# Two exponent arrays and two attention matrices for the heads of branch A, and another order of projections

## The chip, the cores and the metric

The kernel runs on one core of one Trainium2 chip. The metric is the device time of one execution in microseconds, taken as the median of several runs. The engines are named as the profile names them: PE (TensorE) for matmuls, PEld for its weight loads, DVE (VectorE), ACT (ScalarE), POOL (GpSimd) and SP, which issues most transfers.

## The reference

The kernel computes a trunk of two layers over 512 positions of width 1024, in float32. In each layer three branches share one input projection, and a squared-ReLU MLP follows:

```
z  = rms_norm(x) @ w_in          # columns for all branches
A: 4 heads of a gated linear recurrence, forward and backward, state 128 x 128
   log_f, key = gates(z_f, lower bound);  attn[t, s] = sum_k q[t] key[s] exp(b[t] - b[s])
B: u * (W_s @ layer_norm(v) + b_s) in 128-position chunks, 4 groups
C: 8 query heads, 2 key heads, windowed attention |i - j| <= 128, partial rotary, sink logit
merged = sum over branches of sigmoid(gate) * (y_branch @ w_br)
x = x + merged @ w_out;  x = x + relu(rms_norm(x) @ w_up)^2 @ w_down
```

## The kernel before, in words

Everything is tiled to 128 partitions by 512 columns. A float32 product is made from three float32r matmuls: each operand is split in a high and a low part, and high-high, low-high and high-low are added up in PSUM (`mm3`, lines 212 to 214). A weight chunk of 128x1024 is fetched by SP into one of two buffers (tag "wr", line 187), cast to its high part by ACT (line 207) and its low part is made by DVE (line 208). One projection (`proj`) is eight such triples, 24 matmuls, and DVE empties its PSUM bank with a multiplication by the row norm (`evac`, line 708, and line 717 for the gates of a head). Projections use tag "m", two PSUM banks.

The program is written as a trace of operations. A planner with a model of the engines puts them in order: an operation written earlier goes first, `hp()` moves one ahead, and `with later(n)` counts it as if it were written n operations later. Each engine then works through its list in order. Tiles of one tag share a fixed number of buffers, and a new tile waits until one is free.

In each layer a first part multiplies the normed input with the columns that all branches share (`seven`, lines 418 to 420). Then comes the branch stage, which the change is about. Its parts:

- Branch A. `a_ffb(h)` projects the two gates of head h (two projections `f`), then `a_gates` makes an array `ex` of four rows of 128x512: exponents, written by lines 531 and 532 in layer 0, 540 and 548 in layer 1. `a_head` works through seven levels of block size. In each one ACT takes exponentials of `ex` into `qt` (line 572) and `kt` (line 575), DVE multiplies `qt` with the query (line 573), PE forms four 128x128 products (line 558), the result goes into the attention matrix `at` by a masked copy (DVE, line 563) or a copy (ACT, lines 578 and 592), and two additions on DVE update `ex` for the next level (line 600). Behind the levels come the states between chunks (`kd`, `kT`, `stp`, `qd`, lines 606 to 632; line 629 is the last reader of `ex`), the output matmuls (line 643), a norm and a transpose (line 655). `qt`, `kt`, `dg`, `kd`, `qd`, `asq` and `ao` share tag "a" with three buffers. Queries share tag "q" with two.
- Head 0 keeps its `ex` in a four-row tile outside the branch pool (`Z4`), and heads 1 to 3 share one buffer of tag "ex". All heads share one buffer of `at`.
- Branch C projects keys, values and four query groups (`ck`, `cv`, `cq`), rotates them (`rot`: DVE lines 916, 917, 919 and POOL line 918), splits the queries (ACT line 946, DVE line 947), and then runs 16 blocks: scores on PE (lines 963, 964), row maximum, exponentials (ACT line 970), scaling, transposes (`pT`, line 992) and output (`po`, line 997, copied by line 999).
- Branch B ends in eight gate projections `gz` with the projection `yB` beside them (`merge_b(d)`; `fill` calls it with `later(30000)`). They are the work that PE does when nothing else is ready; so are the four output gates `ag` of branch A and the projection `yC` of branch C's output (lines 254 to 256).

The order in which these are written is:

```
ck, cv, cq x4  ->  c_run(0)  ->  head(1): f, f, q and the head  ->  c_run(1..3)
-> fill(0,1,2) -> head(2) -> fill(3,4) -> head(3) -> fill(5,6,7) -> ag x4, yC
```

`c_run` is counted 15000 operations later, `fill` and what follows it 30000. Head 0 is written ahead of all this, its gates already in the part before the stage.

Of the kernel before, what the change touches and what calls it, by code (L numbers as in the profile page):

```python
# [6 lines left out]
F32 = mybir.dt.float32  # L7
# [5 lines left out]
P = 128  # L13
S = 512
# [46 lines left out]
def trunk(tc, xT, xt, ws, vec, fnb, bsb, snk, wst, rope, cmask, amask, ident, out):  # L61
    nc = tc.nc
# [25 lines left out]
    part = {}  # L88
# [4 lines left out]
    def nm(s):  # L93
        ctr[0] += 1
        return f"{s}_{ctr[0]}"

    def T(tag, name, dt=F32):
        where = part[HOME[tag]] if tag in HOME else sb
        return where.tile([P, S], dt, tag=tag, bufs=SLOTS[tag], name=nm(name))
# [11 lines left out]
    def Z4(name):  # L111
        z4[:] = [sb.tile([P, 4, S], F32, tag="z4", bufs=1, name=nm(name)), 0]
        return z4[0]
# [397 lines left out]

    def a_gates(l, h, z2, lbs):

        if h == 0:

            ex, e = Z4("ex"), [T("zt", "ga") for _ in range(2)]
            both = [(e[d], z2[d]) for d in range(2)]
        else:
            ex, e = part["br"].tile([P, 4, S], F32, tag="ex", bufs=1, name=nm("ex")), Z2("ga")
            both = [(e, z2)]  # L520
            e, z2 = [e[:, 0], e[:, 1]], [z2[:, 0], z2[:, 1]]
        lfo = [ex[:, 3], ex[:, 1]]
        for e_, z_ in both:
            nc.scalar.activation(e_, z_, AF.Abs)
        for e_, z_ in both:
            nc.scalar.activation(e_, e_, AF.Exp, scale=-1.0)
        for e_, z_ in both:
            nc.scalar.activation(e_, e_, AF.Ln, bias=onep_t[:, 0:1])
        if l == 0:
            for d in range(2):  # L530
                nc.vector.scalar_tensor_tensor(lfo[d], z2[d], 0.0, e[d], ALU.min, ALU.subtract)
                nc.vector.tensor_tensor(ex[:, 2 * d], lfo[d], z2[d], ALU.subtract)
        else:
            l1p, llb, dl = lbs
            u = e
            for e_, z_ in both:
                nc.vector.scalar_tensor_tensor(e_, z_, 0.0, e_, ALU.min, ALU.subtract)
            for d in range(2):
                c = slice(d * 4 + h, d * 4 + h + 1)
                nc.vector.scalar_tensor_tensor(ex[:, 2 * d], u[d], l1p[:, c], z2[d], ALU.add, ALU.subtract)  # L540
                nc.scalar.activation(z2[d], u[d], AF.Abs, bias=dl[:, c])
                nc.vector.tensor_scalar(u[d], u[d], l1p[:, c], llb[:, c], ALU.add, ALU.max)
            for e_, z_ in both:
                nc.scalar.activation(z_, z_, AF.Exp, scale=-1.0)
            for e_, z_ in both:
                nc.scalar.activation(z_, z_, AF.Ln, bias=onep_t[:, 0:1])
            for d in range(2):
                nc.vector.tensor_tensor(lfo[d], u[d], z2[d], ALU.add)
        return ex

    def a_head(l, h, ex, q, vt):
        at = part["br"].tile([P, 4, P], F32, tag="at", bufs=1, name=nm("at"))

        def attn(kk, qq):
            pt = PT("a", "at")
# [146 lines left out]
    for l in range(DEPTH):  # L702
# [217 lines left out]
            return z  # L920


        lo64, hi64 = slice(0, 64), slice(64, 128)
        ck = evac(proj(xs, "ck", l, "ck"), "ch", "ck")
        cvT = evac(proj(xs, "cv", l, "cv"), "ch", "cv")
# [96 lines left out]
                        c_out(*prev)  # L1022
                    prev = cur

        def head(h):
            g = a_ffb(h)
            q = evac(proj(xs, "q", l, "q", h), "q", "q")
            oa.append(a_head(l, h, g, q, vt))

        prev = None  # L1030
        c_run(0)
        head(1)
        c_run(1)
        c_run(2)
        c_run(3)
        fill(0,1,2)
        with later(15000):
            c_out(*prev)
        head(2)
        fill(3,4)  # L1040
        head(3)
        fill(5,6,7)
        with later(30000):
            for h in range(4):
                gate_a()
# [270 lines left out]
```

## Time and profile before

| | |
|---|---|
| runs, median (lowest to highest) | 1730.86 us (1730.69 to 1731.39), 3 runs |
| profiled execution, span from first to last instruction | 1729.5 us |
| profiled execution's own time | not on the page beside the span; the median of the runs is 1.4 us above the span |
| mean granted clock of TensorE | 0.996 |
| branch stage, layer 0 | about 164 to 448 us |
| branch stage, layer 1 | about 1024 to 1306 us |

Times in the profile count from the first instruction. A line of the timeline gives start, length, engine, line of the code, operation, output and inputs, and in brackets how long the engine stood idle before it and what ended that. A line of the waits gives who waited for whom, the total, how often, and the longest. In the table by stage each engine's busy time stands with its number of instructions in brackets. A matmul's length there includes the time in which it overlaps the next one.

### The profile page before, as it was taken

The page shows a single profiled execution, that of the slowest core. Times are in us where ns is not written, and L with a number is a line of the kernel's source. Part 1 is how long each engine was busy: PE and PEld are TensorE (multiplying, and loading weights), DVE is VectorE, ACT ScalarE, POOL GpSimd, SP SyncE. Part 2 cuts the span into 40 slices and gives each one's busy share as a digit, 9 for nine tenths or more (in the row PEclk, how much of TensorE's full clock was granted, in tenths as well). Part 3 has the DMA queues.
Part 4 walks back from the last instruction along what each step waited for, and adds up shares of the span by engine and source line. Part 5 has one row for each costly group of instructions (what it writes and reads, how often), then busy time and mean ns, then how long its engine had stood idle before and what let it go on. Part 6 is the DMA issues. An engine that isn't in the chain of part 4 may idle for free.

```text
span 1729.5 us, 21976 instructions
## 1 busy us (share of the span) xinstructions
PE 1685.3 (97%) x8024; PEld 1405.0 (81%) x8024; DVE 1297.1 (75%) x2009; ACT 1017.1 (59%) x1715; POOL 146.1 (8%) x215
## 2 busy tenths in 40 slices
PE   8999999999999999999999999999999999999997
PEld 7888878887877888888888787888877878888886
DVE  7996977687566668686889869876776567686867
ACT  7665567677335555545665754877772355545454
POOL 0011200000310000000010112000004000000001
PEclk9999999999999999999999999999999999999999
DMA  8342232231545332233423422322317353232311
GB/s 331 98 146 92 83 104 81 72 104 55 203 187 182 98 110 98 98 98 98 134 92 126 147 93 71 104 79 75 111 48 273 130 182 98 98 98 97 119 65 49
DMA packets 58283, 200.04 MB, mean 116 GB/s; under 512 B 7904, under 2 KB 8288, under 8 KB 58176
## 3 DMA queue, kind: packets, MB, share of 16 engines
q1 hardware_dynamic: 44640, 154.72, 26.6%
q0 software_dynamic: 13248, 43.40, 6.7%
q8 instruction: 63, 1.03, 0.3%
q10 hardware_dynamic: 288, 0.52, 0.1%
q14 instruction: 44, 0.36, 0.1%
HBM read 177.64 MB, written 20.97 MB: 115 GB/s over the span
## 4 chain that ended last, share of the span: by engine, by line
PE 43%; issue 20%; DVE 4%; ACT 2%; POOL 0%; POOLq 0%; ACTq 0%; DVEq 0%
PE up L213 3%; PE up L212 3%; PE up L214 3%; PE dA L418 2%; PE dA L420 2%; PE dA L419 2%; PE at L558 1%; PE gA L418 1%; PE gz L214 1%; PE gz L213 1%; PE gz L212 1%; PE dC L418 1%; PE dC L420 1%; PE dC L419 1%; PE gA L420 1%
## 5 line engine op out<-in xcount | busy, mean ns | idle before, releaser
L207 ACT CAST wh<-wq 128x1024 fp32r<-128x1024 f32 x201 | 211.4, 1052 | 208.2 <-PE up L213 49.3
L208 DVE TENSOR_TENSOR wl<-wq,wh 128x1024 fp32r<-128x1024 f32 x201 | 245.1, 1222 | 117.1 <-ACT wh L207 116.1
L208 DVE TENSOR_TENSOR wl<-wr,wh 128x1024 fp32r<-128x1024 f32 x166 | 203.9, 1228 | 148.0 <-ACT wh L207 147.6
L207 ACT CAST wh<-wr 128x1024 fp32r<-128x1024 f32 x166 | 174.0, 1049 | 214.6 <-PE up L213 67.3
L212 PE MATMUL up<-xh,wh 128*128 128x512 f32 x512 | 199.2, 390 | 1.9 <-ACT u L1171 1.9
L213 PE MATMUL up<-xl,wh 128*128 128x512 f32 x512 | 200.6, 392 | 0.1
L214 PE MATMUL up<-xh,wl 128*128 128x512 f32 x512 | 199.1, 391 | 0.0
L212 PEld LDWEIGHTS up<-xh,wh 128*128 128x128 f32 x512 | 96.3, 188 | 22.7 <-ACT u L1171 2.7
L213 PEld LDWEIGHTS up<-xl,wh 128*128 128x128 f32 x512 | 96.4, 188 | 20.3 <-DVE xl L266 0.6
L214 PEld LDWEIGHTS up<-xh,wl 128*128 128x128 f32 x512 | 96.5, 189 | 19.8
L418 PE MATMUL dA<-wh,sh 128*128 128x512 f32 x256 | 99.8, 390 | 0.0
L419 PE MATMUL dA<-wh,sh 128*128 128x512 f32 x256 | 99.7, 389 | 0.0
L420 PE MATMUL dA<-wl,sh 128*128 128x512 f32 x256 | 92.6, 390 | 0.0
L600 DVE TENSOR_TENSOR ex<-ex 128x512 f32<-128x512 f32 x112 | 78.1, 715 | 6.3 <-ACT kt L575 5.4
L558 PEld LDWEIGHTS at<-qt,kt 128*128 128x128 f32 x448 | 57.0, 191 | 9.9 <-ACT kt L575 4.7
L558 PE MATMUL at<-qt,kt 128*128 128x128 f32 x448 | 59.6, 276 | 5.6 <-DVE qt L573 2.7
L572 ACT ACTIVATE qt<-ex 128x512 f32<-128x512 f32 x56 | 37.7, 674 | 46.3 <-DVE ex L600 38.5
L274 POOL TENSOR_TENSOR rs<-ms,mhalf_t 128x4 f32<-128x4 f32 (+2 forms) x15 | 17.3, 1156 | 530.6 <-DVE ms L272 527.5
L420 PEld LDWEIGHTS dA<-wl,sh 128*128 128x128 f32 x256 | 48.1, 188 | 10.0
L418 PEld LDWEIGHTS dA<-wh,sh 128*128 128x128 f32 x256 | 48.1, 188 | 10.0
L419 PEld LDWEIGHTS dA<-wh,sh 128*128 128x128 f32 x256 | 48.1, 188 | 9.9
L262 ACT CAST sh<-sf 128x512 fp32r<-128x512 f32 x64 | 39.7, 621 | 24.3 <-DVE sf L383 18.0
(403 smaller groups left out, 4403.0 us busy)
## 6 DMA issues: line engine op xcount, KB each, us to landing
wr<-in_ws_dram SPq DMA_DIRECT2D x166, 512.0 KB, 3.3
wq<-in_ws_dram SPq DMA_DIRECT2D x117, 512.0 KB, 4.3
thd<-zt POOLq DMA_DIRECT2D x32, 256.0 KB, 2.5
th<-thd POOLq DMA_DIRECT2D x32, 256.0 KB, 4.6
mgd<-mg POOLq DMA_DIRECT2D x16, 256.0 KB, 2.9
mcd<-th POOLq DMA_DIRECT2D x16, 256.0 KB, 2.5
mC<-mcd POOLq DMA_DIRECT2D x16, 256.0 KB, 6.7
mB<-mgd POOLq DMA_DIRECT2D x16, 256.0 KB, 6.6
```

The source lines that it names most:

```text
L207: nc.scalar.copy(hi, raw)
L208: nc.vector.tensor_tensor(lo, raw, hi.bitcast(F32), ALU.subtract)
L212: nc.tensor.matmul(pt, whi, xhi, start=first, stop=False)
L213: nc.tensor.matmul(pt, whi, xlo, start=False, stop=False)
L214: nc.tensor.matmul(pt, wlo, xhi, start=False, stop=last)
L262: nc.scalar.copy(hi, src)
L418: nc.tensor.matmul(pt, xh[:, t], hi[:, c], start=start and k == 0, stop=False, skip_group_check=True)
L419: nc.tensor.matmul(pt, xl[:, t], hi[:, c], start=False, stop=False, skip_group_check=True)
L420: nc.tensor.matmul(pt, xh[:, t], lo[:, c], start=False, stop=k == 3, skip_group_check=True)
L558: nc.tensor.matmul(pt[:, c], kk(st), qq[:, c], start=True, stop=True)
L572: nc.scalar.activation(qt.rearrange(shp, b=nb, h=2), e_q, AF.Exp)
L600: nc.vector.tensor_tensor(o_ap, o_ap, ap_of(ex, i_, [[istep, 2]] + z), ALU.add)
```

## The change

- `a_gates`: heads 1 and 3 take `ex` from the buffer in the branch pool, heads 0 and 2 from the four-row tile outside it.
- `a_head`: tag "at" has two buffers.
- Head 1's two gate projections and its query are written ahead of branch C's projections. Head 3's three projections are written directly behind head 2.
- The gate groups of branch B are written as (0, 1) ahead of head 2, (2, 3) ahead of head 3, and (4, 5, 6, 7) behind it.
- The scratch space in SBUF that the descriptors of POOL's transfers take is set to 4096 bytes a partition, where before it had its default.

```diff
     def a_gates(l, h, z2, lbs):
 
+        ex = part["br"].tile([P, 4, S], F32, tag="ex", bufs=1, name=nm("ex")) if h % 2 else Z4("ex")
         if h == 0:
 
-            ex, e = Z4("ex"), [T("zt", "ga") for _ in range(2)]
+            e = [T("zt", "ga") for _ in range(2)]
             both = [(e[d], z2[d]) for d in range(2)]
         else:
-            ex, e = part["br"].tile([P, 4, S], F32, tag="ex", bufs=1, name=nm("ex")), Z2("ga")
+            e = Z2("ga")
...
     def a_head(l, h, ex, q, vt):
-        at = part["br"].tile([P, 4, P], F32, tag="at", bufs=1, name=nm("at"))
+        at = part["br"].tile([P, 4, P], F32, tag="at", bufs=2, name=nm("at"))
...
+        def project(h):
+            return a_ffb(h), evac(proj(xs, "q", l, "q", h), "q", "q")
+
+        def head(h, g, q):
+            oa.append(a_head(l, h, g, q, vt))
+
+        head_1 = project(1)
         lo64, hi64 = slice(0, 64), slice(64, 128)
         ck = evac(proj(xs, "ck", l, "ck"), "ch", "ck")
...
-        def head(h):
-            g = a_ffb(h)
-            q = evac(proj(xs, "q", l, "q", h), "q", "q")
-            oa.append(a_head(l, h, g, q, vt))
-
         prev = None
         c_run(0)
-        head(1)
+        head(1, *head_1)
         c_run(1)
         c_run(2)
         c_run(3)
-        fill(0,1,2)
+        fill(0, 1)
         with later(15000):
             c_out(*prev)
-        head(2)
-        fill(3,4)
-        head(3)
-        fill(5,6,7)
+        head(2, *project(2))
+        head_3 = project(3)
+        fill(2, 3)
+        head(3, *head_3)
+        fill(4, 5, 6, 7)
...
-    nc = _bacc.Bacc("TRN2", target_bir_lowering=False, num_devices=1)
+    nc = _bacc.Bacc("TRN2", target_bir_lowering=False, num_devices=1, dynamic_dma_scratch_size=4096)
```

## The prediction

> **What bounds the kernel now.** I read the head of the page, then the kernel cut into its stages, then TensorE's waits, then the order of time at the two places where TensorE stands still.
>
> ```profile
> span 1729.5 us, 21976 instructions
> PE 1685.3 (97%) x8024; PEld 1405.0 (81%) x8024; DVE 1297.1 (75%) x2009; ACT 1017.1 (59%) x1715; POOL 146.1 (8%) x215
> ```
>
> TensorE is busy for 97% of the span, and the change takes no matmul away. A busy share can hide a slow rate, so the rate comes first: how far apart are two matmuls of one line, with two others between them?
>
> ```profile
> 214.73 0.39 PE L212 MATMUL f<-xh,wh 128*128 128x512 f32 x1
> 215.41 0.39 PE L212 MATMUL f<-xh,wh 128*128 128x512 f32 x1
> ```
>
> Three matmuls in 0.68 us, 0.227 us each, though one is shown as 0.39: they overlap, and back to back they run at this pace through nearly the whole trace. So the only time to be had is where TensorE waits, and the change can only reach the branch stages. Busy time by stage, layer 0 in three pieces, then layer 1 (length, then PE, PEld, DVE, ACT, POOL, granted clock, DMA):
>
> ```profile
> 164.40:225.00 60.60, 57.57 (x283) 48.24 (x282) 54.93 (x81) 29.37 (x43) 13.82 (x11) 0.97 0.31 104
> 225.00:404.00 179.00, 178.64 (x970) 153.67 (x969) 129.65 (x296) 128.65 (x285) 14.23 (x20) 1.00 0.27 90
> 404.00:448.00 44.00, 38.08 (x230) 32.51 (x229) 32.89 (x70) 30.35 (x81) 5.53 (x8) 1.00 0.21 73
> 1024.00:1090.00 66.00, 61.57 (x306) 51.40 (x304) 60.94 (x89) 34.66 (x53) 12.46 (x11) 0.97 0.29 95
> 1090.00:1268.00 178.00, 178.00 (x972) 153.77 (x971) 133.23 (x288) 140.54 (x297) 15.97 (x21) 1.00 0.27 89
> 1268.00:1306.00 38.00, 34.44 (x205) 29.60 (x204) 28.11 (x60) 26.18 (x72) 3.55 (x7) 1.00 0.23 84
> 200.00:225.00 25.00, 22.09 (x104) 18.36 (x103) 24.75 (x35) 12.24 (x19) 4.48 (x3) 0.93 0.21 75
> 1075.00:1100.00 25.00, 21.41 (x104) 17.99 (x103) 22.69 (x42) 18.33 (x36) 1.64 (x2) 0.93 0.24 78
> ```
>
> Idle TensorE: at the start of the stage 3.03 and 4.43 us (7.46), in the middle 0.36 and 0, at the end 5.92 and 3.56 (9.48). A granted clock of 0.93 in 25 us is a further 1.75 us lost behind each start, 3.5 for two. Together 20.4 us, 1.2% of the span, are the most that this change can win. There is no such ceiling on what it can lose. The middle is full in both layers, with VectorE and ScalarE at some 72 to 79%.
>
> Who is waited for?
>
> ```profile
> PE q L212 <- DVE z L717: 4.9, 2, 2.9
> PE po L997 <- ACT pT L993: 3.1, 2, 1.7
> PE at L558 <- DVE qt L573: 2.7, 2, 1.6
> PE at L558 <- ACT kt L575: 2.5, 3, 1.8
> ```
>
> The starts are one story: head 1's query projection waits until VectorE has emptied head 1's gate projections out of PSUM.
>
> ```profile
> 216.09 0.28 PE L963 MATMUL sc<-k,q 128*128 128x256 f32 x1
> 219.67 0.80 PE L212 MATMUL q<-xh,wh 128*128 128x512 f32 x1 [2.91 <-DVE z L717]
> 214.74 3.55 DVE L947 TENSOR_TENSOR q<-cq,q 64x512 fp32r<-64x512 f32 x5
> 218.33 0.69 DVE L917 TENSOR_TENSOR sh<-sh,sin 128x512 f32<-128x512 f32 x1
> 218.94 0.68 DVE L717 TENSOR_TENSOR z<-f,rb 128x512 f32<-128x512 f32 x1
> ```
>
> VectorE, 24.75 us busy in 25, is in the rotations and splits of branch C (L917, L947) when the evacuation L717 is wanted. The ends are another story: head 3 and the last blocks of branch C are chains over all engines, and nothing else is left for TensorE.
>
> ```profile
> 427.74 1.56 PE L997 MATMUL po<-pT,cvt 128*128 128x256 f32 x6 [1.42 <-ACT pT L993]
> 432.43 1.16 PE L558 MATMUL at<-qt,kt 128*128 128x128 f32 x8 [1.80 <-ACT kt L575]
> 436.54 0.93 PE L620 MATMUL stp<-vt,kT 128*128 128x128 f32 x6 [1.76 <-ACT kT L617]
> 437.55 0.70 PE L254 MATMUL yC<-wh,yh 128*128 128x512 f32 x2
> ```
>
> The projection of C's output goes on at 437.55, after both.
>
> **The change, part by part.**
>
> *Head 1's two gate projections and its query ahead of C's six.* Each is 24 matmuls of 0.227 us: 3 x 24 x 0.227 = 16.3 us of TensorE go forward, and C's 6 x 24 x 0.227 = 32.7 us go back by as much. With each go a weight transfer on SP's queue, a cast on ScalarE and a subtraction on VectorE, in the order of the projections; so three transfers pass six. The sum of the work is the same. L717 now stands ahead of the rotations in VectorE's queue, not behind them, so the wait of 2.91 us goes. What is late next: the rotations run 16 us later, and whatever projection follows C's then meets the same crowded VectorE, with the first gates of B in the place of head 1's query. VectorE also gets head 1's gates and first levels into this piece. A level costs it one L573 and two L600, and a masked copy:
>
> ```profile
> L573 DVE TENSOR_TENSOR qt<-qt,q x56: 669/686/1779, 174.0 to 1288.9; 128x512 f32<-128x512 f32 x56
> L600 DVE TENSOR_TENSOR ex<-ex x112: 670/685/1787, 177.5 to 1290.1; 128x512 f32<-128x512 f32 x112
> L563 DVE COPY_PREDICATED at<-amask_t,at x40: 717/732/756, 185.8 to 1285.7; 128x512 f32<-128x512 uint8 x40
> ```
>
> That is 0.69 + 2 x 0.69 + 0.73 = 2.8 us a level. Bounds for the two starts: the wait goes with the clock behind it (-7.5 - 3.5 = -11.0), or two levels pushed in ahead of an evacuation in one layer add 5.6 us. I take half of what is there, -5.5: the cause moves away from head 1, but VectorE's work in this stretch isn't less. [...] In the row of 200 to 225 us a wait of 2.91 us was enough to bring the clock to 0.93. [...]
>
> *Two exponent arrays in turn.* Heads 0 and 2 take the array outside the branch pool, heads 1 and 3 the one inside it. Does a head wait for that array now? Rows between 300 and 336 us, the handover from head 1 to head 2 (last column but one: first and last start):
>
> ```profile
> L629 ACT ACTIVATE qd<-ex x2: 525/527/529, 306.2 to 307.5; 128x384 f32<-128x384 f32 x2
> L532 DVE TENSOR_TENSOR ex<-ex,z x2: 683/684/684, 310.9 to 311.5; 128x512 f32<-128x512 f32 x2
> L643 PE MATMUL av<-vt,at x8: 271/276/276, 317.3 to 324.2; 128*128 128x128 f32 x8
> L572 ACT ACTIVATE qt<-ex x1: 858/858/858, 330.4 to 330.4; 128x512 f32<-128x512 f32 x1
> L578 ACT COPY at<-at x1: 585/585/585, 334.6 to 334.6; 128x512 f32<-128x512 f32 x1
> ```
>
> Head 2's exponents are written as soon as head 1 has read its own for the last time (307.5), so the array does hold them up. But they are ready at 312.2, and the first level starts at 330.4, 18 us later, behind head 1's output matmuls (324.2): tag "a" has three buffers for qt, kt, qd and the rest, and head 1's two qd hold two of them until those matmuls. So the second array alone doesn't shorten the handover. What it allows is that levels of the next head slip in among those of the head before, where both queries and gates are there early. *Two attention matrices* are what such mixing needs: the next head's first copy (L578, 334.6) comes 10 us after the old matrix is free, so by itself the second matrix is worth nothing, and costs nothing.
>
> *Head 3's projections behind head 2's, gates of B later.* Three projections (16.3 us) pass gate projections that have the same length and follow them instead; their three transfers on SP and the gates' stores on POOL's queue swap places in the same way. The sum is unchanged, and the full middle hides it. Were that cover gone, the price would be at the buffers: tag "q" has two, so head 3's query can leave PSUM only when head 1's has been read for the last time (just behind L629, 307.5), and until then one of the two "m" banks is held with the gates queued behind it; six gates that wait for one evacuation of 0.69 us each are 4 us a layer. I put it at 0, since head 1's levels come earlier too. What the move can bring is at the end of the stage.
>
> ```profile
> 416.28 1.16 PE L558 MATMUL at<-qt,kt 128*128 128x128 f32 x8 [0.18 <-ACT kt L575]
> 433.42 1.03 PE L997 MATMUL po<-pT,cvt 128*128 128x256 f32 x4
> ```
>
> Head 3's levels come every 4.0 us there (from 416.28 to 432.43 in four steps). If two of its seven have gone ahead among head 2's, its last one comes 8 us earlier; but C's last block (L997, 433.42) is the other chain, and that gets only the room on ScalarE and VectorE that head 3 leaves. Bounds: all of the 9.48 us goes, or C comes later, which is the second rival below. I take four tenths, -3.8, near the small end, because of two chains only one is shortened.
>
> *Four kilobytes for the descriptors of POOL's transfers.* It makes the room for the second matrix; no instruction changes, and I put it at 0. The bound is the third rival.
>
> *New gaps.* Two heads and C share three engines and the three buffers of tag "a"; that is a new reason for waits of the kind of L558 <- L573 (1.35 us each). One of them: +1.5.
>
> Sum: -5.5 - 3.8 + 1.5 = -7.8, a span of 1721.7. The page gives only a span for its execution, and the median of the runs, 1730.86, is 1.4 above it; with the same 1.4 the forecast is **1723.1, say 1723**. Its own range is 1717 (the starts gone by 9, the ends by half) to 1727.
>
> **The rivals.**
>
> *All waits go.* If mixing the heads shortens the chains by 10 us or more and VectorE keeps up, 18 of the 20.4 us are won: 1731 - 18 = 1713. For it: the idle time at the ends is spread over gaps of 2 us and less, so a little lead fills them. Against it: VectorE's 24.75 us in 25 at the start.
>
> *Nothing overlaps: the change doesn't do what it says.* Head 2's exponents lay ready for 18 us and the start waited for tag "a"; if those three buffers also keep the levels apart, the second array and matrix only let gates run earlier, and the stalls move without shrinking: 1731, within 3.5 us either way (0.2%, about what a measurement of this kernel can tell from no change).
>
> *Branch C becomes the last chain: slower.* Place: C's scores. They start once its projections are in and rotated, and these go back by 16.3 us, so the first score moves from 216.09 towards 232. And C gives way to the heads' projections on TensorE, as L964 shows in two stretches (length, PE busy and count, PEld, clock, DMA):
>
> ```profile
> 261.00:288.00 27.00, 0.12 (x1) 0.00 (x0) 1.00 0.21 69
> 310.00:336.00 26.00, 0.00 (x0) 0.00 (x0) 1.00 0.24 82
> ```
>
> One score matmul in 53 us. With heads 2 and 3 projected together these two pauses become one, which may give back some 8 us of the 16, so C ends some 8 us later, at 441 in place of 433, and so in layer 1. At the end TensorE already stands still, so a delay of C is a delay of the yC projection behind it, us for us. Half of it comes back if head 3, done earlier, leaves C its room: 2 x 4 = +8, 1739; none of it comes back: +16, and the gain of the starts (-5.5) against that brings it to +10.5, 1741. It decides if the first score comes later than about 224 us and C doesn't regain it by its third run. For it: C has the lower priority and ends last now. Against it: in the last third head 3 leaves it room.
>
> *POOL's transfers wait for room.* Place: the bursts behind the branch stage.
>
> ```profile
> 466.98 2.43 POOL L1075 DMA_DIRECT2D mB<-mgd  x4
> mB<-mgd POOLq DMA_DIRECT2D x16, 256.0 KB, 6.6
> ```
>
> POOL issues four in 2.43 us, 0.61 each, and each takes 6.6 us to land, so about eleven are under way; if the space held fewer, issue would wait for a landing, 6.6 us once in each layer less what is hidden: +10 us, 1741. Nothing in the trace shows such a wait. [...]
>
> **How the numbers follow.** Forecast 0.45, all waits gone 0.12, nothing overlaps 0.12, C last 0.27, POOL's transfers 0.04. Faster by over 0.2%: 0.45 + 0.12 = 0.57; within 0.2%: 0.12; slower: 0.27 + 0.04 = 0.31. The likeliest single case gives 1723. The range runs from 1711, just below the case in which all waits go, to 1741, which takes in C at 1739 and its bound; beyond these I leave two in ten: starts that lose more than two levels, C with the whole 16 us, or two bad cases at once.
>
> **What would show it.** Right: no wait of `q` for L717 in the first stretch of either stage, and fewer than 11 us of idle TensorE and lost clock left there; gates of head 2 written (L531, L532) before head 1's last L629; L558 of head 3 between levels of head 2; less than 6 us idle in the two end windows together. Wrong: head 2's first L572 still behind head 1's L643 with no level before it (nothing overlaps); L997 of the last block later than now relative to the first yC matmuls, with yC waiting for L262 or L999 (C last); a slice of clock below 1.00 in the middle of the stage, which has none now; POOL's issues spread over more time in the burst behind the stage. If the starts have lost their wait to another evacuation, L708 or L901, by as much, the term of -5.5 is the one that failed.

## The result, and the profile after

| | median | lowest to highest | runs |
|---|---|---|---|
| before, beside it on the same chip | 1730.78 us | 1726.91 to 1731.42 | 6 |
| after | 1735.09 us | 1734.30 to 1735.80 | 6 |

The ratio is 1.0029, with a 95% interval of 1.0017 to 1.0040: the changed kernel is 4.3 us slower, where 1723 us, 8 us faster, had been forecast. In the changed kernel the lines behind L513 have moved by one and those of branch C by eight: the level's L572, L575 and L558 are now L573, L576 and L559, the evacuations L708 and L717 are L709 and L718, the rotation's L917 is L918, C's L964 and L997 are L972 and L1005.

The head of the page of the changed kernel, and its stages (length, then PE, PEld, DVE, ACT, POOL, granted clock, DMA). Layer 1 is cut 2.8 us later than before, since all of it starts that much later; the last two rows are the output part behind each branch stage.

```profile
span 1733.8 us, 21981 instructions
PE 1690.0 (97%) x8024; PEld 1406.4 (81%) x8024; DVE 1301.9 (75%) x2009; ACT 1022.1 (59%) x1717; POOL 147.4 (9%) x215
...
164.40:225.00 60.60, 60.44 (x311) 51.18 (x310) 54.79 (x80) 37.33 (x57) 13.05 (x10) 1.00 0.33 113
225.00:404.00 179.00, 175.12 (x947) 150.06 (x946) 135.23 (x294) 123.11 (x267) 18.74 (x22) 0.99 0.26 87
404.00:448.00 44.00, 39.23 (x221) 32.98 (x220) 31.10 (x75) 30.96 (x87) 4.00 (x7) 1.00 0.15 55
1026.80:1092.80 66.00, 66.00 (x341) 56.30 (x340) 61.37 (x87) 46.66 (x68) 12.43 (x11) 1.00 0.30 97
1092.80:1270.80 178.00, 173.13 (x933) 147.53 (x932) 136.01 (x288) 128.54 (x276) 15.62 (x21) 0.99 0.26 87
1270.80:1308.80 38.00, 33.70 (x190) 28.78 (x189) 25.09 (x60) 27.63 (x76) 2.31 (x4) 0.96 0.11 36
225.00:250.00 25.00, 22.96 (x115) 19.23 (x114) 20.91 (x46) 13.51 (x34) 3.95 (x4) 0.93 0.25 85
1092.00:1117.00 25.00, 21.79 (x106) 17.98 (x105) 20.50 (x45) 12.22 (x30) 2.90 (x4) 0.93 0.26 85
460.00:500.00 40.00, 37.74 (x175) 29.83 (x174) 25.25 (x36) 10.65 (x14) 14.95 (x28) 1.00 0.77 281
1320.00:1365.00 45.00, 42.74 (x197) 33.84 (x196) 28.12 (x41) 11.99 (x15) 16.86 (x32) 1.00 0.76 280
```

The same two last stretches of the kernel before:

```profile
460.00:500.00 40.00, 38.47 (x180) 30.74 (x180) 27.01 (x38) 11.21 (x14) 15.27 (x29) 1.00 0.80 300
1320.00:1365.00 45.00, 43.48 (x203) 34.87 (x202) 29.18 (x41) 12.57 (x16) 13.46 (x26) 1.00 0.69 268
```

Idle TensorE and lost clock, each term of the forecast beside what these rows give (us):

| | before | after | change | forecast |
|---|---|---|---|---|
| the two starts | 7.46 + 3.5 | 0.16 + 2.04 + 3.21, + 3.5 | -2.0 | -5.5 |
| the middle of the stages | 0.36 | (3.88 - 2.04) + (4.87 - 3.21) = 3.50 | +3.1 | 0, and +1.5 for new gaps |
| the ends | 9.48 | 4.77 + 4.30, + 0.04 x 38 = 1.5 | +1.1 | -3.8 |
| behind the stages | 3.05 | 4.52 | +1.5 | not in the sum |

Together +3.7 of the 4.3 by which the span is longer; the other 0.6 us is not placed by these stretches. The sum agrees, but not layer by layer: the same rows give +0.2 in layer 0 and +3.4 in layer 1. Layer 1 begins 2.8 us late all the same, because the granted clock of 500 to 600 us is 0.98 where the kernel before has 1.00, some 2 us; later the kernel before loses some 1.4 us in the same way (0.99 in 1365 to 1500 us) and the changed one doesn't. Falls of the clock come and go between executions (in 200 to 225 us it is 0.93 in the kernel before and 1.00 in e1_scratch, last section), so the terms of clock here, 3.5 us at the starts and 1.5 at the ends, are those of one execution of each kernel.

The starts still have their wait. TensorE's waits, and the place in layer 0 (start, length, engine, line, operation; idle before it in brackets):

```profile
PE gz L212 <- DVE gz L709: 5.0, 2, 2.9
...
PE mT L1076 <- DVE mB L1081: 3.4, 6, 0.7
```

```profile
227.18 2.17 POOL L919 TENSOR_TENSOR cq<-cq,cos 128x512 f32<-128x512 f32 x1 [3.75 <-DVE sh L917]
...
228.11 1.79 DVE L918 TENSOR_TENSOR sh<-sh,sin 128x512 f32<-128x512 f32 x1
229.94 2.12 DVE L955 TENSOR_TENSOR q<-cq,q 64x512 fp32r<-64x512 f32 x3
...
233.01 2.12 DVE L955 TENSOR_TENSOR q<-cq,q 64x512 fp32r<-64x512 f32 x3
...
235.43 0.68 DVE L709 TENSOR_TENSOR gz<-gz,rb 128x512 f32<-128x512 f32 x1
...
236.17 0.68 PE L212 MATMUL gz<-xh,wh 128*128 128x512 f32 x1 [2.04 <-DVE gz L709]
236.65 0.63 PE L213 MATMUL gz<-xl,wh 128*128 128x512 f32 x1
237.08 0.63 PE L214 MATMUL gz<-xh,wl 128*128 128x512 f32 x1
```

The wait of the query for L717 (4.9 us) is now a wait of branch B's gates for L709 (5.0 us), behind the same rotations and splits on VectorE, and the clock is lost behind it as before: the matmuls from 236.65 on are 0.43 us apart, not 0.23.

Branch C's scores, L972 in one stretch of each layer (length, PE busy and count, PEld, clock, DMA), then the end of layer 0:

```profile
253.00:293.50 40.50, 0.81 (x3) 0.58 (x4) 1.00 0.26 85
1117.00:1148.00 31.00, 0.37 (x2) 0.14 (x2) 1.00 0.28 94
```

```profile
425.80 1.16 PE L559 MATMUL at<-qt,kt 128*128 128x128 f32 x8 [0.66 <-ACT kt L576]
...
438.11 1.13 PE L1005 MATMUL po<-pT,cvt 128*128 128x256 f32 x4 [0.46 <-ACT pT L1001]
...
441.00 1.17 PE L254 MATMUL yC<-wh,yh 128*128 128x512 f32 x4
```

The two pauses of C have become one. Head 3's last level is 6.6 us earlier than before (425.80 against 432.43), and C's last block 4.7 us later (438.11 against 433.42); yC goes on behind it, at 441.00 in place of 437.55.

In layer 0 the late C costs TensorE little, since other matmuls stand in the gap: idle in the end window are 4.77 us in place of 5.92, and by the end of that window it has done four matmuls less than before (311 + 947 + 221 against 283 + 970 + 230), some 0.9 us. In layer 1 the last matmul of C's last block starts 9.3 us later (1303.2 against 1293.9), of which 2.8 are the layer's later start; there the end loses 2.3 us more than before, 1.5 of them clock.

### The profile page after: what moved, and what is told of

Its sections match the earlier page's. It is cut to its first block, busy times and chain, and to the rows that moved or that the text cites. A ratio compares the mean times of both kernels' runs of the same rounds, so it can differ in the third digit from the quotient of the medians.

```text
span 1733.8 us, 21981 instructions
## 1 busy us (share of the span) xinstructions
PE 1690.0 (97%) x8024; PEld 1406.4 (81%) x8024; DVE 1301.9 (75%) x2009; ACT 1022.1 (59%) x1717; POOL 147.4 (9%) x215
## 4 chain that ended last, share of the span: by engine, by line
PE 60%; issue 25%; ACT 6%; DVE 5%; DMA 2%; POOL 1%; POOLq 0%; SPq 0%; DVEq 0%; ACTq 0%
PE up L212 3%; PE up L213 3%; PE up L214 3%; PE at L559 2%; PE po L1005 2%; PE wo L255 2%; PE dA L418 2%; PE dA L420 2%; PE dA L419 2%; PE wo L254 2%; PE wo L256 2%; PE gz L212 2%; PE gz L213 2%; PE gz L214 2%; PE av L644 1%
## 5 line engine op out<-in xcount | busy, mean ns | idle before, releaser
L213 PEld LDWEIGHTS up<-xl,wh 128*128 128x128 f32 x512 | 96.5, 188 | 20.4 <-DVE xl L266 0.5
L559 PEld LDWEIGHTS at<-qt,kt 128*128 128x128 f32 x448 | 57.4, 191 | 8.1 <-ACT kt L576 3.7
L559 PE MATMUL at<-qt,kt 128*128 128x128 f32 x448 | 59.5, 275 | 3.3 <-ACT kt L576 2.2
L212 PE MATMUL gz<-xh,wh 128*128 128x512 f32 x128 | 52.1, 407 | 5.0 <-DVE gz L709 5.0
```

Of the source, the lines that this page charges most:

```text
L212: nc.tensor.matmul(pt, whi, xhi, start=first, stop=False)
L213: nc.tensor.matmul(pt, whi, xlo, start=False, stop=False)
L559: nc.tensor.matmul(pt[:, c], kk(st), qq[:, c], start=True, stop=True)
```

## The experiments

Unless a base is named, the edits are made to the kernel before. "C" and "head 3" in the table are the starts, in layer 0's timeline, of the last matmul of C's last output block and of head 3's last level; where rows of several matmuls are shown, these begin up to 0.9 us earlier. Each ratio is to runs of the kernel before beside it on the same chip. The intervals are about 0.1% to either side, some 2 us, so a difference of 1 or 2 us between two experiments decides nothing.

| kernel | C | head 3 | median, us | ratio to before, 95% interval |
|---|---|---|---|---|
| e2_head1 | 429.2 | 428.5 | 1724.2 | 0.9958, 0.9944 to 0.9971 |
| e26_head1_rotdve | 428.8 | 423.2 | 1724.6 | 0.9967, 0.9955 to 0.9980 |
| e23_head1_later | 430.0 | 429.3 | 1725.1 | 0.9968, 0.9957 to 0.9980 |
| e9_no_order3 | 429.9 | 429.1 | 1725.6 | 0.9972, 0.9960 to 0.9984 |
| e19_head3_after_c | 433.0 | 430.1 | 1728.7 | 0.9988, 0.9979 to 0.9997 |
| e21_both_after_c | 430.6 | 429.8 | 1729.1 | 0.9993, 0.9983 to 1.0002 |
| e12_head1_a6 | 433.6 | 407.8 | 1729.9 | 0.9993, 0.9985 to 1.0002 |
| e7_after_rotdve | 437.4 | 425.9 | 1729.9 | 0.9996, 0.9987 to 1.0005 |
| before | 434.1 | 433.3 | 1730.8 | |
| e22_head3_a6 | 435.5 | 416.3 | 1733.1 | 1.0014, 1.0005 to 1.0023 |
| e18_regroup | 435.3 | 434.6 | 1733.6 | 1.0017, 1.0008 to 1.0025 |
| after | 438.9 | 426.7 | 1735.1 | 1.0029, 1.0017 to 1.0040 |
| e5_after_a6 | 436.9 | 410.6 | 1736.2 | 1.0032, 1.0020 to 1.0044 |
| e24_c_first | 426.8 | 432.5 | 1738.4 | 1.0040, 1.0026 to 1.0054 |

**Which part costs?** Four kernels with one part of the change each, then two that leave one part out.

e1_scratch: POOL's descriptors alone.

```diff
-    nc = _bacc.Bacc("TRN2", target_bir_lowering=False, num_devices=1)
+    nc = _bacc.Bacc("TRN2", target_bir_lowering=False, num_devices=1, dynamic_dma_scratch_size=4096)
```

> The kernel before with nothing but the scratch for POOL's transfers at 4096 bytes; the order of instructions on every engine is the same as before. Theory 1 (the loss is in the order of the branch stage): the same time as before, within 1 us. Theory 2 (POOL's transfers wait for room): slower by some 4 us, with POOL's bursts behind the branch stage (about 457 to 485 us) stretched.

1729.41 us, ratio 0.9994 (0.9983 to 1.0004), with the instructions of every engine in the order of before. The smaller scratch costs nothing, and the rival of POOL's transfers falls.

e2_head1: head 1's projections alone.

```diff
+        head_1 = project(1)
         lo64, hi64 = slice(0, 64), slice(64, 128)
         ck = evac(proj(xs, "ck", l, "ck"), "ch", "ck")
...
-        head(1)
+        head(1, *head_1)
```

> The kernel before with head 1's three projections ahead of branch C's, nothing else. Theory 1a (the wait at the start only moves to the first gates of B, and C starts 16 us later): idle TensorE at the start stays at 2 to 4 us a layer, the first score moves to about 232 us, the whole is within 3 us of before. Theory 1b (this edit is what costs): slower by 4 us or more, with the added idle at the end of the stage.

1724.22 us (1722.78 to 1724.47): 7 us faster than before, more than either side expected, and the fastest kernel of this study. Its end of layer 0:

```profile
427.57 1.16 PE L558 MATMUL at<-qt,kt 128*128 128x128 f32 x8 [1.80 <-ACT kt L575]
428.56 1.03 PE L1004 MATMUL po<-pT,cvt 128*128 128x256 f32 x4
```

Both chains end 4.9 us earlier than before, side by side. C's first score is 15 us later here too (231 us), but C regains that: head 2's and head 3's projections still come apart, each behind its gates of B, and C's largest pause is 16.9 us, not 27.8. The wait at the starts has also gone to the gates (gz for L708, 4.5 us).

e3_arrays: two exponent arrays and two attention matrices, with the small scratch.

```diff
+        ex = part["br"].tile([P, 4, S], F32, tag="ex", bufs=1, name=nm("ex")) if h % 2 else Z4("ex")
...
-        at = part["br"].tile([P, 4, P], F32, tag="at", bufs=1, name=nm("at"))
+        at = part["br"].tile([P, 4, P], F32, tag="at", bufs=2, name=nm("at"))
```

> The kernel before with the two exponent arrays in turn, two attention matrices and the smaller scratch, in the old order of projections. Theory 1 (three buffers of tag a keep the heads apart, so the arrays are worth nothing): head 2's exponents are written well before head 1 is done, yet its first level still starts behind head 1's output matmuls, and the time is within 2 us of before. Rival (the arrays let levels mix): levels of head 2 among those of head 1, 4 to 8 us faster.

1731.69 us, ratio 1.0001 (0.9992 to 1.0010). Alone the arrays are worth nothing. Head 2's exponents are there at 287 us, and its first level starts at 334, behind head 1's output matmuls (320 to 327), as the theory has it.

e4_order3: head 3's projections behind head 2 and the gates of B regrouped, with one array and one matrix.

```diff
-        fill(0,1,2)
+        fill(0, 1)
...
-        head(2)
-        fill(3,4)
-        head(3)
-        fill(5,6,7)
+        head(2, *project(2))
+        head_3 = project(3)
+        fill(2, 3)
+        head(3, *head_3)
+        fill(4, 5, 6, 7)
```

> The kernel before with head 3's projections behind head 2's and the gates of B regrouped, one exponent array and one matrix, head 1's projections in the old place. Theory 1c (the move by itself is what costs, since branch C stands still behind 33 us of projections): a wait of TensorE in the middle of the stage and a later end of C, 3 to 5 us slower. Rival (order is neutral, since the sum is the same): within 2 us.

1750.01 us, ratio 1.0103 (1.0088 to 1.0118): 18.7 us slower. C's last block comes at 443.0 us, and here the middle breaks open too (a stretch of the stages, and VectorE):

```profile
285.00:309.00 24.00, 17.53 (x100) 13.93 (x99) 18.29 (x50) 18.34 (x53) 0.60 (x1) 0.93 0.14 51
```

```profile
305.07 1.29 DVE L531 SCALAR_TENSOR_TENSOR ex<-z,ga 128x512 f32<-128x512 f32 x2
306.55 1.28 DVE L532 TENSOR_TENSOR ex<-ex,z 128x512 f32<-128x512 f32 x2
308.81 1.28 DVE L717 TENSOR_TENSOR z<-f,rb 128x512 f32<-128x512 f32 x2
```

Head 3's two gate projections are done at 284 us, and their evacuation L717 runs at 308.81, behind the writing of head 2's exponents (L531, L532): the array is head 1's until then, and head 3's gates stay in PSUM meanwhile. Both banks of tag "m" are held for 25 us, head 3's query and the gates of B stand queued behind them, and TensorE is idle for 6.5 us.

e8_no_head1: the whole change without head 1's move.

```diff
-        head_1 = project(1)
...
-        head(1, *head_1)
+        head(1, *project(1))
```

> The changed kernel with head 1's projections put back behind branch C's: two arrays, two matrices, head 3's projections behind head 2's. If the parts add up (head 1 first: -7; the whole: +4), it is 11 us slower than before, 1742, with TensorE idle in the middle of the stage. Rival (the two moves of projections only hurt each other): within 3 us of before.

1732.76 us, ratio 1.0013 (1.0002 to 1.0023). With the arrays the move of head 3 and the gates costs 1.4 us beside before; without them it cost 18.7. Head 3's gates are evacuated at 280.73 and 284.89 us here (L718), right behind their projections, and TensorE is busy for all of 285 to 309 us. The arrays pay for that move, and the parts don't add.

e9_no_order3: the whole change with the old order of head 3 and the gates.

```diff
-        fill(0, 1)
+        fill(0,1,2)
...
-        head_3 = project(3)
-        fill(2, 3)
-        head(3, *head_3)
-        fill(4, 5, 6, 7)
+        fill(3,4)
+        head(3, *project(3))
+        fill(5,6,7)
```

> The changed kernel with head 3's projections and the gates of B in the old order: head 1's projections first, two arrays, two matrices. If the move of head 3's projections is what costs, this is about as fast as the kernel with head 1's move alone, 1724 to 1726, with no idle TensorE between 260 and 400 us. Rival (the arrays cost something once head 1 comes early): 1730 or more.

1725.55 us. So in the changed kernel the move of head 3 and the gates costs 1735.09 - 1725.55 = 9.5 us, more than all that it is slower.

```profile
428.21 1.16 PE L559 MATMUL at<-qt,kt 128*128 128x128 f32 x8 [1.79 <-ACT kt L576]
429.20 1.03 PE L1005 MATMUL po<-pT,cvt 128*128 128x256 f32 x4
```

**Is it the buffers of head 3's gates?** Five buffers of tag "z2" in place of three, in the changed kernel and in e4_order3 (there with the small scratch).

```diff
-    WR, WB, NZ, NCT, NSM, NQ = 2, 3, 3, 4, 3, 10
+    WR, WB, NZ, NCT, NSM, NQ = 2, 3, 5, 4, 3, 10
```

> The changed kernel with five buffers in place of three for gate projections and keys (tag z2). Theory (head 3's gate projections wait in PSUM for such a buffer, and the gates of B are queued behind them): the evacuations L718 of head 3 come within 2 us of the end of their projections, the idle time in the middle of the stage (1.8 us in layer 0, about 4.5 in layer 1) goes, 3 to 6 us faster than the changed kernel, about 1730. Rival (C's pause behind six projections in a row is the cause, or another order altogether): the time of the changed kernel, 1735.

> The kernel before with head 3's projections behind head 2's and the gates regrouped, one exponent array and one matrix, but five buffers of tag z2 in place of three (and the small scratch, which made no difference). Theory (both banks of tag m were held from 284 to 309 us because head 3's gates found no z2 buffer): the evacuations L717 follow their projections, the idle 25 us in the middle of the two stages fall below 8, and the time comes to 1731 to 1736 from 1750. Rival (six projections in a row are the cause, whatever the buffers): it stays at 1745 or more.

e14: 1734.07 us, within the noise of the changed kernel, as the rival has it. e15: 1742.85 us, 7 us less than e4_order3 and between the two times put down. In layer 0 its theory fails:

```profile
285.00:309.00 24.00, 18.02 (x101) 14.44 (x100) 19.40 (x52) 19.59 (x56) 1.14 (x2) 0.93 0.13 43
...
307.12 1.28 DVE L717 TENSOR_TENSOR z<-f,rb 128x512 f32<-128x512 f32 x2
```

Head 3's gates are still evacuated only at 307.12, behind the writing of head 2's exponents, and TensorE is idle for 6.0 us. In layer 1 that evacuation comes at 1168 us in place of 1179, and the idle time of 1155 to 1180 us falls from 6.5 to 3.0 us. So it is not the buffers of "z2" that hold the banks in layer 0; what frees them there is the second array (e8_no_head1). The rest of e4's loss was not taken apart.

**Is it the heads, kept apart by tag "a"?** Six buffers of tag "a", in the changed kernel and in e2_head1.

```diff
-             "q": 2, "a": 3, "g": 2, "ch": 10,
+             "q": 2, "a": 6, "g": 2, "ch": 10,
```

> The changed kernel with six buffers of tag "a" in place of three. Theory (the three buffers keep the heads of branch A apart, so that the second array and matrix can't work): head 2's exponents, ready at about 278 us, are followed by its first level before head 1's output matmuls (312 to 318 us), head 3's levels come among head 2's, and the kernel is 3 to 8 us faster than the changed one: 1727 to 1732. Rival (the order of priorities or ScalarE and VectorE keep them apart, not the buffers): the first level of head 2 still follows head 1's output matmuls and the time stays at 1735 within 1.5 us.

> The kernel before with head 1's projections ahead of branch C's, the small scratch, and six buffers of tag "a". Theory (the buffers keep head 1's levels behind head 0's too, and that part of the change has the room for more): 1719 to 1722, under the 1724 of that part alone. Rival (the heads are kept apart by their one exponent array here, or VectorE sets the pace): 1724 within 1.5 us; if levels get ahead of branch C's blocks, more than 1726.

e5: 1736.18 us, as the rival has it; e12: 1729.86 us, 5.6 us more than e2_head1, the last case of its expectation: head 3's last level comes at 407.8 us, and C's last block at 433.6 in place of 429.2. First the changed kernel: head 2's exponents are there at 278 us, head 1 ends at 317, head 2's first level comes behind that.

```profile
276.69 1.29 DVE L533 TENSOR_TENSOR ex<-ex,z 128x512 f32<-128x512 f32 x2
...
317.15 0.39 PE L644 MATMUL av<-st,qd 128*128 128x128 f32 x2
...
319.70 0.88 ACT L573 ACTIVATE qt<-ex 128x512 f32<-128x512 f32 x1
```

With six buffers (end of layer 0, and a wait):

```profile
409.80 1.05 PE L559 MATMUL at<-qt,kt 128*128 128x128 f32 x8
...
436.17 1.13 PE L1005 MATMUL po<-pT,cvt 128*128 128x256 f32 x4 [0.82 <-ACT pT L1001]
...
PE mT L1076 <- DVE mC L1097: 5.5, 2, 3.0
```

Head 3's last level is 16 us earlier than in the changed kernel and the time is no shorter: branch A's chain isn't the one that ends the stage. C's is, and its lateness reaches into the next part, where the transposes wait for C's product (mC, 5.5 us). The buffers do keep the heads from running ahead, but even here head 2's first level (307.0) follows head 1's output matmuls (298.8 to 304.4): they don't mix.

**Is it branch C?** e18_regroup and e19_head3_after_c undo one half of the move each, in the changed kernel: the first puts gates 2 and 3 back between the two heads' projections, the second lets head 3's projections give way to C's scores.

```diff
-        head_3 = project(3)
         fill(2, 3)
-        head(3, *head_3)
+        head(3, *project(3))
```

> The changed kernel with gates 2 and 3 of branch B ahead of head 3's projections, so that these are not directly behind head 2's; gates 4 to 7 stay behind head 3. Theory (it is the six projections in a row that cost, by one pause of branch C of 39.5 us and by head 3's gates held in PSUM): two pauses of under 30 us again, the last block of C at about 430 us, and 1726 within 2 us. Rival (it is the other grouping of the gates that costs, 2+2+4 in place of 3+2+3): 1733 to 1735.

1733.55 us, the rival's time: only 1.5 us of the 9.5 come back. In layer 0 C has pauses under 20 us again (18.6 us the largest), so six projections in a row are not by themselves what costs. C's last block only comes back to 435.3 us. Head 2's projections stand ahead of the third gates here as in the changed kernel, begin at 247 us where e9_no_order3 begins them at 260, and keep C's fourth group of scores until 272 us (there 252). So the grouping of the gates, which the rival named, decides when the heads' projections get ahead of C's scores; that this is what costs is read from the trace here, and the next run tests it.

```diff
-        head_3 = project(3)
+        with later(15000):
+            head_3 = project(3)
```

> The changed kernel with head 3's three projections at a lower priority than branch C's scores, in the same place of the program. Theory (the loss is branch C: its one pause of 39.5 us makes its last block late, 438.9 in place of 429.9 us): the pause shrinks to about 20 us, the last block comes at about 430 us, and 1726 to 1729. Rival (the loss is in the buffers that head 3's gates and query hold, whenever they come): the pause shrinks, but the time stays above 1732.

1728.73 us, within the theory's range: 6.4 us come back by a change of priority alone, with the groups of gates as in the changed kernel. C's largest pause is 18.3 us, but its last block had been expected at 430 us. L972 in the stretch of the pause, and the end:

```profile
250.00:293.50 43.50, 2.10 (x7) 1.33 (x7) 0.96 0.24 79
...
429.20 1.16 PE L559 MATMUL at<-qt,kt 128*128 128x128 f32 x8 [0.34 <-ACT kt L576]
...
432.25 1.13 PE L1005 MATMUL po<-pT,cvt 128*128 128x256 f32 x4 [1.03 <-ACT pT L1001]
```

C's last block is 5.9 us earlier in layer 0 and 9.0 in layer 1 (1294.2 against 1303.2, of which 4 are that layer's earlier start); head 3's last level is 3.4 us later.

e24_c_first: C ahead of the projections of heads 2 and 3 altogether, in the changed kernel.

```diff
         def c_run(j):
             nonlocal prev
-            with later(15000):
+            with later(0):
```

> The changed kernel with branch C's runs ahead of the projections of heads 2 and 3 in priority (they stand behind them in the changed kernel). Theory (branch C is the last chain of the branch stage, and its lateness is the loss): its largest pause falls under 20 us, its last block comes before 430 us, and the time is 1722 to 1728. Rival (C's lateness only goes along with another cause): C ends earlier, and the time stays above 1732. Third possibility: C ends so early that head 3 is the last chain; then the last L559 comes after 435 us, and the time is 1728 to 1735.

1738.36 us, slower than the changed kernel. By what was put down this is the rival, not the theory: C ends earlier and the time stays above 1732. The third possibility has the last chain right, but neither its place (behind 435 us) nor its time.

```profile
426.12 1.03 PE L1005 MATMUL po<-pT,cvt 128*128 128x256 f32 x4
...
431.69 1.13 PE L559 MATMUL at<-qt,kt 128*128 128x128 f32 x8
...
454.13 1.10 PE L656 MATMUL oT<-id_t,ao 128*128 128x128 f32 x4 [3.35 <-DVE ao L652]
```

C ends 12 us earlier than in the changed kernel, and TensorE is idle for 1.6 us in 404 to 448 us in place of 4.8. But now head 3 is last; its norm and transpose are waited for (3.35 us here, 2.2 in layer 1). It isn't all of it: layer 1's middle also has a wait of 2.9 us of yB for an evacuation L709 and a clock of 0.97 in 1157 to 1217 us, and its end (1268 to 1325 us) a clock of 0.94. So an early C alone doesn't win. The runs fit a stage that ends with the later of two chains that share all engines: in the fast orders of e2_head1 and e9_no_order3 both chains end together and early. That this is all that counts is not shown; e21_both_after_c, next, has both at 430 us too and is slower.

e21_both_after_c, e22_head3_a6 and e23_head1_later: head 2's projections at C's priority as well; e19_head3_after_c with six buffers of tag "a"; e2_head1 with head 3's projections at C's priority.

```diff
-        head(2, *project(2))
+        with later(15000):
+            head_2 = project(2)
+        head(2, *head_2)
```

> The changed kernel with the projections of heads 2 and 3 both at branch C's priority, so behind its scores. Theory (C last): last block of C before 430 us, 1723 to 1727, a little under the 1729 that head 3's alone gave. Rival (from here on head 2 and 3 come too late, so that the end of the stage belongs to head 3): 1729 to 1736.

> The changed kernel with head 3's projections behind C's scores, and six buffers of tag "a". Theory (with C no longer late, the earlier end of head 3 that six buffers bring counts): 1722 to 1727, under the 1729 without the buffers. Rival (heads that run ahead take ScalarE and VectorE from C, so C is last again): C's last block after 434 us and 1729 to 1735.

> The kernel before with head 1's projections ahead of branch C's (1724), and head 3's projections behind C's scores. Theory (C is the last chain there too, with its last block at 429 us): 1720 to 1723. Rival (head 3 is the last chain there, its last L558 at 428 us as late as C's block): 1724 to 1728.

e21: 1729.14 us, the rival's number but not its reason, since head 3's last level is at 429.8 and C ends at 430.6; what holds it above e9_no_order3 was not found. e22: 1733.10 us, the rival: head 3's last level is at 416.3, and C is last at 435.5; that it is ScalarE and VectorE which the heads take from it was not shown. e23: 1725.08 us, the rival too: where both chains end together, giving C the way wins nothing.

**What is the wait at the start?** The rotation's multiplication by the cosine on VectorE in place of POOL, in the changed kernel and in e2_head1.

```diff
-            nc.gpsimd.tensor_tensor(z, z, cos_t, ALU.mult)
+            nc.vector.tensor_tensor(z, z, cos_t, ALU.mult)
```

> The changed kernel with the rotation's multiplication by the cosine on VectorE in place of POOL. Theory (VectorE's crowd at the start is made by the two engines slowing each other: 1.78 us for L917 beside POOL, 0.69 us alone): a rotation takes VectorE 1.4 us in place of 1.8 for the two multiplications, the wait of gz for L709 falls under 2 us in each layer, and 1731 to 1733. Rival (the crowd is the sum of VectorE's work, to which this adds): the wait stays 2.5 us or more in each layer, and the time 1735 or above.

> The kernel before with head 1's projections ahead of branch C's (1724), and the rotation's multiplication by the cosine on VectorE. Theory (as in the changed kernel): the wait for L708 falls under 2 us in each layer, 1720 to 1723. Rival: the wait stays, 1724 to 1727.

e7: 1729.85 us, 5.2 us less than the changed kernel and below the range of its theory. The rotation's other multiplication, mean ns of one, before, after, and in e7; then e7's wait in layer 1 (there is none in layer 0) and its first stretch:

```profile
L917 DVE TENSOR_TENSOR sh<-sh,sin 128x512 f32<-128x512 f32 x10 | 8.6, 864 | 0.1
```

```profile
L918 DVE TENSOR_TENSOR sh<-sh,sin 128x512 f32<-128x512 f32 x10 | 13.4, 1341 | 0.1
```

```profile
L918 DVE TENSOR_TENSOR sh<-sh,sin 128x512 f32<-128x512 f32 x10 | 6.9, 686 | 0.1
...
PE gz L212 <- DVE gz L709: 0.8, 1, 0.8
...
225.00:250.00 25.00, 25.00 (x135) 21.51 (x134) 20.87 (x55) 15.11 (x38) 2.15 (x3) 1.00 0.25 85
```

VectorE does more and is done sooner, and at the start the wait and the lost clock are gone. C's last block stays late in layer 0 (437.4), so this is a cost of its own beside C's. This is the cause of the term that failed at the start: the crowd there is not only VectorE's work, it is also what VectorE's instructions take beside POOL's multiplication, and the change made that more (864 to 1341 ns in the mean of these lines; 686 in e7). e26: 1724.64 us, no better than e2_head1, though its start is full as well (0.5 us of wait in layer 1): the end of layer 1 and the output parts lose what the start wins, 4.2 us idle in 460 to 500 us with a clock of 0.96, against 1.5 us and 1.00 in e2_head1. No version of these beats e2_head1.

## Why the prediction was wrong

- *What bounds it, and the ceiling of 20.4 us:* nothing here speaks against it; the largest gain of any kernel is 7 us. In sum over both layers 3.7 of the 4.3 us are waits and clock in the branch stages and right behind them.
- *The starts, -5.5:* the step that failed is "L717 now stands ahead of the rotations, so the wait goes", with half of it kept for what is late next. The query's wait did go (0.3 us is left of q for L718). The next evacuation in line, L709 of B's first gates, waits as long (5.0 us), and loses the same 3.5 us of clock: -2.0. The text named this ending as the test of the term. It took VectorE's load for the cause, with 0.69 us for L917, and didn't ask what that instruction takes beside POOL; e7_after_rotdve shows what that was worth. Its own lines had a sign of it: L573 and L600 take up to 1.78 and 1.79 us where the typical one takes 0.69; at 183.50 and 1060.88 us one of each takes 1.78, both beside a multiplication of POOL.
- *The ends, -3.8:* the step that failed is that an earlier head 3 shortens the end. The idle time there went from 9.48 to 9.07 us, and with 1.5 us of lost clock in layer 1 the term is +1.1. Head 3's chain did come 6.6 us earlier in layer 0, but without any mixing of levels, so that this is near the 8 that were worked out is luck. A chain that is shortened while another ends later gives nothing. e5_after_a6 shows it at its plainest: 16 us earlier, nothing won.
- *Buffers at 0 and new gaps at +1.5:* the middle lost 3.1 us in place of 1.5. The price of held PSUM banks was real where only the order is changed (e4_order3), but what they wait behind in layer 0 is the one exponent array and not "q", and five buffers of "z2" leave that as it is (e15_order3_z5); the second array takes nearly all of the cost away (e8_no_head1). Most of what is left in layer 0 falls into the pause of C: at 277 us TensorE waits 1.53 us for head 1's kt, with no score of C to fill the gap.
- *Behind the stage:* +1.5, not in the sum; that the change can only reach the branch stages was too narrow. The transposes mT wait for mB six times (3.4 us in the row above; before, twice, 1.3 us). That a late C reaches into this part is shown for mC in e5_after_a6 alone.
- *The scratch, 0:* right (e1_scratch). That POOL's issues wait for room, the 0.04 in the sum of the chances, is shown by no run; with the smaller scratch alone the time was 1729.41 us. *The arrays by themselves, 0:* right (e3_arrays), but worth 17 us where head 3's projections come early (e4_order3 against e8_no_head1, the arrays and the scratch together): "costs nothing, wins nothing" held only for the old order.
- *The rivals:* "branch C becomes the last chain" is what happened, by its own steps: the first score at 231.66 us (towards 232), two pauses made one (39.5 us), C's last block later, and the threshold of 224 us passed. Its price was too high, +8 to +10.5 against +4.3. (The +8 leaves out the gain of the starts that the +10.5 counts; with it the lower end is +2.5, and the measured time lies between.) C lost 4.7 us in layer 0, not 8, and "us for us" failed: TensorE lost only some 0.9 us of that there, and most of the loss is in layer 1. Its cause was put in the wrong place: head 1's move delays the first score as much in e2_head1, where C regains it all. What it doesn't regain are projections of heads that stand ahead of its scores: with head 3's behind them 6.4 of the 9.5 us come back (e19_head3_after_c), while keeping them ahead and only breaking the row of six gives 1.5 (e18_regroup). The time lies inside the range given, on its slow side. That rival had 0.27 and the forecast 0.45; two chains with 1 us between them (432.43 and 433.42) and one of them pushed back should have reversed this.

Still open: why the late C costs so much less in layer 0 than in layer 1, where the rest of the 9.5 us goes, why e21_both_after_c stays 3.5 us above e9_no_order3 with both chains at 430 us, and the rest of e4_order3's loss.

## What to carry to other kernels

Where a stage ends with two chains, find the last step of each in the timeline before any gain is given for shortening one; work that is taken forward for the one is taken from the other, and a lower priority for that work can win more than its earlier place. A wait that is taken from one projection on a crowded engine goes to the next one in the queue; ask what makes the crowd, and whether the engine's own instructions are longer there than elsewhere. Parts of a change that are worth nothing alone can be worth 17 us under another part, so leave one out as well as putting one in.

## What was unexpected in the hardware

VectorE's instructions were longer beside POOL's. In the rows of the start POOL's multiplication (227.18, 2.17 us long, where the shortest of its ten takes 1.29) ends at 229.35, and VectorE's L918, shown from 228.11 and 1.79 us long, ends at 229.90, 0.55 us behind it; in e7_after_rotdve, where POOL multiplies nothing in the rotation, its mean is 0.69 us. It looks as if its work had begun only about when POOL was done: an estimate from these two numbers, which agree within some 0.1 us (0.55 against 0.69). Why was not shown. By e7_after_rotdve it was worth 5 us to this kernel (1729.85 against 1735.09), and by e26_head1_rotdve nothing to e2_head1 (1724.64 against 1724.22).

The clock falls behind some short waits and not behind others. In the changed kernel the wait of 2.04 us at 236.17 is followed by matmuls 0.43 us apart, at a granted clock of 0.53 in 236.2 to 238 us. In the kernel before a longer one, 2.28 us, is not; the matmuls behind it go on 0.23 us apart, at a clock of 1.00 in 538.2 to 540 us:

```profile
537.81 0.66 PE L327 MATMUL xT<-id_t,xr 128*128 128x128 f32 x4 [2.28 <-DVE xl L266]
538.22 0.48 PE L213 MATMUL up<-xl,wh 128*128 128x512 f32 x1
538.54 0.39 PE L214 MATMUL up<-xh,wl 128*128 128x512 f32 x1
538.77 0.39 PE L212 MATMUL up<-xh,wh 128*128 128x512 f32 x1
```

Length alone doesn't decide it; what does was not shown. For e1_scratch, with the same instructions in the same order as before, the profiled span was 1724.4 us against 1729.5, with a clock of 1.00 in 200 to 225 us where before shows 0.93. So one profile can't decide a difference of a few us here, and the times above rest on repeated runs.
